# All merge gates of the second block kept in DRAM, their products spread over the three branches' steps

## The chip, the core and the metric

The kernel runs on one core of one Trainium2 chip. The time is device microseconds (us) of one launch: 2844.17 us, the median of 3 runs (2843.86 to 2845.45). The core has a matrix engine (TensorE, PE in the profile; PEld is its weight load), a vector engine (VectorE, DVE), an activation engine (ScalarE, ACT), GpSimd (POOL), and a queue that only issues DMAs (SyncE, SP). Each engine takes its instructions in the order in which they were written into its queue when the program was built, and waits on semaphores for data of the others.

## The reference

A first block (attention, FFN, a linear recurrence, FFN) is followed by a second block of two layers. The change lies in the second block alone. For x of 512 tokens by 1024 channels, each layer computes

```
h = rmsnorm(x, norm_g[l]);  z = h @ w_in[l]
(nsa_q, nsa_kv, nsa_gate, nsa_silu, fox_qkv, fox_f, fox_silu, mem_q, mem_silu, merge_g) = split(z)
o_a = nsa(...) * silu(nsa_silu)        # 8 heads: compressed, selected and window attention
o_b = fox(...) * silu(fox_silu)        # 8 heads: causal attention with a decay
o_m = memory_xattn(...) * silu(mem_silu)   # 4 heads over 256 memory rows
g = sigmoid(merge_g)                   # 3 gates of 512 x 1024
u = g[0] * (o_a @ w_branch_a) + g[1] * (o_b @ w_branch_b) + g[2] * (o_m @ w_branch_m)
x = x + u @ w_out[l]
```

The three gates are one product of h with 3072 columns of w_in; they depend on h alone, not on the branches.

## The kernel before

All products run as three float32r matmuls (`mm3`, L45 to L47): high part by high part, high by low, low by high. A weight tile is loaded from DRAM by SP (`ws`), rounded by ACT (`wh`) and its rest taken by DVE (`wl`), L204 and L212; there are 2 buffers of `ws` and 4 of `wh` and `wl`.

In a layer of the second block three generators run one after the other: `memory`, `nsa` and `fox`. Each yields after a step. `nsa` has 40 steps: 20 blocks of projections, 4 of compressed probabilities, and 16 of heads (one half of the queries of one head each, here called a head step). `fox` has 40 steps too: twice 12 of projections and 8 head steps. In a head step PE computes scores (`sc`, L1160, L1161 in nsa, L1324, L1325 in fox), DVE adds the mask and takes the minimum (L888), ACT the exponential (L889), POOL scales (L891), PE turns the tile (`tr`, L856), ACT and DVE split it (`pt`, L204), and PE multiplies by the values (`pv`, L916). At the end of two heads DVE multiplies by the silu (L940) and the result is split into `o`.

`weave` runs the main generator, and after step n takes as many steps of a filling generator as n stands in the plan (`PLANS`). The filler before is `branch`, one for each branch: a gate's product takes two steps of 12 matmuls (`acc<-hH,wh`, 128x512), then its tanh goes into a tile `mt` in SBUF (L1027; 2 buffers), and one step of 12 matmuls gives one eighth of the branch's output product (`acc<-o,wh`); DVE multiplies it by the gate (L1043, L1046), POOL adds it to `u` (L1047). A branch has 24 filling steps, 72 a layer. A branch's gates and products alternate, so a gate is held in SBUF for a step or two only.

The order written so is not the one in the queues: a scheduler at build time moves an instruction ahead of others whose data are not ready. What stands in the queues is shown below where the change moves it. Products need one of three PSUM banks `acc`; a bank is free when DVE or ACT has read it.

Of the kernel before, what the change touches and what calls it, by code (L numbers as in the profile page):

```python
# [10 lines left out]
F32 = mybir.dt.float32  # L11
# [6 lines left out]
T = 512  # L18
D = 1024
NT = T // 128  # L20
KD = D // 128
# [4 lines left out]
WINDOWS = (128, 512, 2048)  # L26
NB_U = 384
BANKS = {"acc": 3, "sc": 2, "tr": 2, "pv": 1}
SEC_BUFS = {"st": 7, "ws": 2, "w": 4, "o": 6, "P": 5, "pt": 4, "zc": 3, "hst": 4, "fox_t": 4, "of": 2, "rt": 2, "sl": 2, "mt": 2, "cst": 2, "ct": 2}
LRU_BUFS = 24  # L30
NORMALIZE_AFTER, VALUES_AFTER = 5, 6
LRU_STEPS = (0, 1, 2, range(4), "v", 3, range(4, 8), "vvv")
PLANS = ((16,),
         (8, 13, 13, 14, 15, 18, 19, 19, 22, 22, 25, 26, 26, 27, 27, 28, 28, 29, 29, 35, 35, 37, 38, 39),
         (1, 5, 5, 8, 8, 10, 12, 15, 16, 17, 19, 21, 32, 32, 34, 35, 38))
TURN_BANKS = (("acc", "sc"), ("acc", "sc"), ("sc", "tr"), ("tr", "pv"))
TOK_BANKS = (("acc", "acc", "acc", "pv"), ("sc", "sc", "tr", "tr"), ("acc", "acc", "acc", "sc"), ("sc", "tr", "tr", "sc"))

# [4 lines left out]
def mm3(nc, out, lh, ll, rh, rl, start, stop):  # L43

    nc.tensor.matmul(out, lh, rh, start=start, stop=False)  # L45
    nc.tensor.matmul(out, lh, rl, start=False, stop=False)  # L46
    return nc.tensor.matmul(out, ll, rh, start=False, stop=stop)  # L47


@contextmanager  # L50
def behind(tc, *ins):

    with ExitStack() as st:
        for i in ins:
            if i is not None:
                st.enter_context(tc.issue_after(i.ins))
        yield
# [111 lines left out]
class Net:  # L169
# [739 lines left out]
    def pv(self, ps, first, last, v, pts, half):  # L909

        nc = self.nc
        nj = 2 * half + 2
        for j in range(nj):
            lo = 128 if j == nj - 1 else 0
            for u, p in enumerate(pts):
                nc.tensor.matmul(ps[:, lo:256], v(j), p[:, j, lo:], start=first and j == 0 and u == 0, stop=last and j == nj - 1 and u == 1)  # L916

    def merge_halves(self, of, ps, e, half):

# [37 lines left out]
    def second_layer(self, l, z2):  # L957
        nc, i, tc = self.nc, self.i, self.tc
        w_in, h = i["w_in_2"][l], self.h
        with tc.tile_pool(name=f"sec{l}", bufs=1) as self.lp:  # L960
            lp = self.lp
            u, o_m, o_a, o_b = [], [], [], []
            br = [self.branch(l, h, o, i[f"w_branch_{x}_2"][l], b, u) for o, x, b in ((o_m, "m", 2), (o_a, "a", 0), (o_b, "b", 1))]
            self.weave(self.memory(l, h, w_in, z2, o_m), br[0], PLANS[0])
            self.weave(self.nsa(l, h, w_in, o_a), itertools.chain(br[0], br[1]), PLANS[1])
            self.weave(br[0])
            self.weave(self.fox(l, h, w_in, o_b), itertools.chain(br[1], br[2]), PLANS[2])
            self.weave(br[1])
            self.weave(br[2])
            uh = []  # L970
            for k in range(0, KD, 2):
                s = self.state([128, 2, 2, T])
                for q in range(2):
                    self.split(s[:, q, 0], s[:, q, 1], u[k // 4][:, k % 4 + q], scale=0.5)
                uh.append(s)
            lh = lambda k, t: uh[k // 2][:, k % 2, 0, t * 128:(t + 1) * 128]
            ll = lambda k, t: uh[k // 2][:, k % 2, 1, t * 128:(t + 1) * 128]
            last = l == 1
            dst = self.out[0] if last else self.x_new()
            w = i["w_out_2"][l]  # L980
            y0 = list(self.tm(w, 0, 512, lh, ll))
            y1 = self.tm(w, 512, 512, lh, ll, banks=1, tail=4)
            gn = None
            if not last:
                gn = self.lt("o", [128, D])
                nc.sync.dma_start(gn, i["norm_g_2"][l + 1][None, :].to_broadcast([128, D]))

            def new_x(t, *ys):
                xt = self.lt("o", [128, D])
                nc.sync.dma_start(xt, self.x[t * 128:(t + 1) * 128])  # L990
                for c, y in enumerate(ys):
                    cs = slice(c * 512, c * 512 + 512)
                    nc.vector.tensor_tensor(xt[:, cs], xt[:, cs], y, op=OP.add)
# [12 lines left out]
            return gen  # L1006

    def branch(self, l, h, o, w, b, u):

        nc = self.nc  # L1010
        kt = 4
        wv = w.rearrange("(k p) c -> p k c", p=128)
        first = not u
        ts = []

        wg = self.i["w_in_2"][l].rearrange("(k p) c -> p k c", p=128)

        def gate(m):
            c = OFF_MG + b * D + m * 128
            wh, wl = self.wunit(wg[:, :, c:c + 128])  # L1020
            pg = self.bank()
            for k in range(KD):
                mm3(nc, pg, wh[:, k], wl[:, k], h[0][:, k], h[1][:, k], k == 0, k == KD - 1)
                if k == KD // 2 - 1:
                    yield
            t = self.lt("mt", [128, T])
            nc.scalar.activation(t, pg, AF.Tanh, scale=0.5)  # L1027
            ts.append(t)
            yield

        yield from gate(0)
        for m in range(KD):
            if m + 1 < KD:
                yield from gate(m + 1)
            wh, wl = self.wunit(wv[:, :, m * 128:(m + 1) * 128])
            ps = self.bank()
            for k in range(kt):
                mm3(nc, ps, wh[:, k], wl[:, k], o[k][:, 0], o[k][:, 1], k == 0, k == kt - 1)
            t = ts[m]
            if first:  # L1040
                if m % 4 == 0:
                    u.append(self.state([128, 4, T], F32))
                nc.vector.scalar_tensor_tensor(u[m // 4][:, m % 4], t, 1.0, ps, op0=OP.add, op1=OP.mult)  # L1043
            else:
                um = u[m // 4][:, m % 4]
                nc.vector.scalar_tensor_tensor(t, t, 1.0, ps, op0=OP.add, op1=OP.mult)  # L1046
                nc.gpsimd.tensor_tensor(um, um, t, op=OP.add)  # L1047
            yield
# [493 lines left out]
```

## Time and profile before

| what | value |
|---|---|
| median of 3 runs | 2844.17 us |
| the profiled execution | 2847.33 us, of which span 2845.2 us |
| granted TensorE clock, mean | 0.988 |
| PE busy | 2752.4 us (97%) |
| ACT busy | 1285.5 us (45%) |
| DVE busy | 1655.0 us (58%) |
| DMA | 288.52 MB, mean 101 GB/s |

The second block's two layers fill the span from about 1550 us to its end: the first to 2204 us, the second after it. A busy PE is not PE at its full pace: a matmul counts as busy until its last column is out, so short matmuls that wait for each other show little idle time. So the stretches are read by how many matmuls of which size go through in how many us. The column PEclk of the windows is the granted clock: 1.00 is 2.4 GHz, and stretches at half of it run at 1.2 GHz.

### The profile page before, as it was taken

Reading aid. Unit: us, or ns where it says so; the run is one execution under the profiler, and the core shown is the slowest. Engines: PE = TensorE matmul, PEld = TensorE weight load, DVE = VectorE, ACT = ScalarE, POOL = GpSimd, SP = SyncE. Lnnn points to the kernel's source line nnn. Section 1 sums busy time; section 2 is a strip of 40 time slices with the busy share of each in tenths; the row PEclk is TensorE's granted clock in tenths of the full one; section 3 lists DMA queues with packets and bytes.
Section 4 is the critical chain, followed back from the end, with each engine's and each line's share of the span. In section 5 each row is a group of like instructions: output and inputs, shape, how many; then the busy total and the mean of one; then the engine's idle time right before and its main releaser. Section 6 shows DMA issues by size and latency. Waiting matters only on the chain.

```text
span 2845.2 us, 39405 instructions
## 1 busy us (share of the span) xinstructions
PE 2752.4 (97%) x14493; PEld 2338.7 (82%) x14493; DVE 1655.0 (58%) x3306; ACT 1285.5 (45%) x2518; POOL 509.2 (18%) x682
## 2 busy tenths in 40 slices
PE   7999999799999998999998999999999899999999
PEld 6788888688888887888887898789878798788987
DVE  3245555555542678555425687776744677777753
ACT  3234344344432465444323554666533554665542
POOL 0001101111100000111001242333320242333420
PEclk9999999899999999999999999999999999999999
DMA  5553443333332343433323424122234423113233
GB/s 172 171 169 86 104 94 86 118 111 97 97 126 96 112 122 108 126 96 97 126 97 114 125 74 109 38 54 75 71 93 141 137 70 109 34 46 84 71 93 107
DMA packets 386071, 288.52 MB, mean 101 GB/s; under 512 B 33576, under 2 KB 339496, under 8 KB 385880
## 3 DMA queue, kind: packets, MB, share of 16 engines
q1 hardware_dynamic: 376752, 268.94, 32.9%
q10 hardware_dynamic: 9128, 17.07, 1.6%
q8 instruction: 115, 1.88, 0.3%
q14 instruction: 76, 0.62, 0.1%
HBM read 266.86 MB, written 21.20 MB: 101 GB/s over the span
## 4 chain that ended last, share of the span: by engine, by line
PE 82%; DVE 8%; DMA 4%; ACT 3%; issue 2%; POOL 1%; SPq 0%; ACTq 0%; DVEq 0%; POOLq 0%
PE acc L45 20%; PE acc L46 20%; PE acc L47 20%; PE tr L856 2%; PE sc L45 2%; PE sc L46 2%; PE sc L47 2%; DVE wl L204 2%; PE pv L916 2%; PE tr L45 2%; PE tr L47 1%; PE tr L46 1%; PE pv L46 1%; PE pv L47 1%; DMA ws<-in_attn_w_qkv_dram 1%
## 5 line engine op out<-in xcount | busy, mean ns | idle before, releaser
L204 DVE TENSOR_TENSOR wl<-ws,wh 128x1024 fp32r<-128x1024 f32 (+2 forms) x476 | 563.9, 1186 | 686.8 <-ACT wh L204 680.8
L204 ACT CAST wh<-ws 128x1024 fp32r<-128x1024 f32 (+2 forms) x476 | 469.5, 987 | 819.7 <-PE acc L46 303.6
L45 PE MATMUL acc<-hH,wh 128*128 128x512 f32 (+1 forms) x1928 | 742.3, 386 | 12.2 <-ACT gate L769 6.2
L46 PE MATMUL acc<-hL,wh 128*128 128x512 f32 (+1 forms) x1928 | 741.3, 385 | 1.5 <-DVE hL L204 1.2
L47 PE MATMUL acc<-hH,wl 128*128 128x512 f32 (+1 forms) x1928 | 739.5, 384 | 1.0 <-DVE wl L204 1.0
L45 PEld LDWEIGHTS acc<-hH,wh 128*128 128x128 f32 x1928 | 363.3, 189 | 83.6 <-ACT gate L769 6.6
L47 PEld LDWEIGHTS acc<-hH,wl 128*128 128x128 f32 x1928 | 363.9, 189 | 69.2 <-DVE wl L204 1.5
L46 PEld LDWEIGHTS acc<-hL,wh 128*128 128x128 f32 x1928 | 364.1, 189 | 68.4 <-DVE hL L204 2.5
L45 PE MATMUL acc<-wh,hH 128*128 128x256 f32 (+3 forms) x864 | 267.3, 312 | 5.4 <-ACT hH L204 4.1
L46 PE MATMUL acc<-wl,hH 128*128 128x256 f32 (+3 forms) x864 | 266.9, 310 | 2.3 <-DVE wl L204 2.3
L47 PE MATMUL acc<-wh,hL 128*128 128x256 f32 (+3 forms) x864 | 264.9, 309 | 0.1
L45 PEld LDWEIGHTS acc<-wh,hH 128*128 128x128 f32 x864 | 165.6, 192 | 14.5 <-ACT hH L204 4.5
L46 PEld LDWEIGHTS acc<-wl,hH 128*128 128x128 f32 x864 | 165.7, 192 | 11.9 <-DVE wl L204 3.7
L47 PEld LDWEIGHTS acc<-wh,hL 128*128 128x128 f32 x864 | 165.3, 191 | 7.4 <-DVE hL L204 0.4
L645 POOL TENSOR_TENSOR cv<-cv 128x512 f32<-128x512 f32 x48 | 62.0, 1292 | 465.1 <-DVE cv L582 448.4
L582 DVE SCALAR_TENSOR_TENSOR cv<-acc,cw,cv 128x511 f32<-128x511 f32 (+1 forms) x192 | 142.5, 746 | 3.2
L856 PE MATMUL tr<-ident,P 128*128 128x128 f32 x720 | 123.3, 277 | 10.7 <-DVE pt L204 5.2
L817 POOL TENSOR_TENSOR hst<-hst,mhalf 128x4 f32<-128x4 f32 (+2 forms) x90 | 91.0, 1017 | 223.5 <-DVE hst L816 221.7
L889 ACT ACTIVATE P<-P,soft 128x128 f32<-128x128 f32 (+1 forms) x192 | 108.1, 563 | 49.9 <-DVE soft L888 45.7
L888 DVE CUSTOM_DVE_ANT_0 P<-sc,causal 128x128 f32<-128x128 f32 (+1 forms) x192 | 92.9, 486 | 45.8 <-PE tr L856 31.5
L891 POOL TENSOR_SCALAR P<-P,soft,ngate 128x128 f32<-128x128 f32 (+3 forms) x128 | 83.9, 658 | 153.6 <-DVE soft L890 117.5
L204 DVE TENSOR_TENSOR pt<-tr,pt 128x128 fp32r<-128x128 f32 (+2 forms) x224 | 104.1, 474 | 11.8 <-ACT pt L204 10.4
(452 smaller groups left out, 4770.1 us busy)
## 6 DMA issues: line engine op xcount, KB each, us to landing
ws<-in_w_in_dram SPq DMA_DIRECT2D x116, 512.0 KB
ws<-in_ffn_w_up_dram SPq DMA_DIRECT2D x96, 512.0 KB
ws<-in_attn_w_qkv_dram SPq DMA_DIRECT2D x72, 512.0 KB
ws<-in_ffn_w_down_dram SPq DMA_DIRECT2D x48, 512.0 KB
x<-x ACTq DMA_DIRECT2D x16, 512.0 KB
ws<-in_lru_w_in_dram SPq DMA_DIRECT2D x16, 512.0 KB
ws<-in_w_mem_kv_dram SPq DMA_DIRECT2D x16, 512.0 KB
ws<-in_w_out_dram SPq DMA_DIRECT2D x16, 512.0 KB
```

Source lines behind the costliest of these rows:

```text
L45: nc.tensor.matmul(out, lh, rh, start=start, stop=False)
L46: nc.tensor.matmul(out, lh, rl, start=False, stop=False)
L47: return nc.tensor.matmul(out, ll, rh, start=False, stop=stop)
L204: return nc.scalar.copy(hi, src), (eng or nc.vector).tensor_tensor(lo, src, hi.bitcast(F32), op=OP.subtract)
L582: nc.vector.scalar_tensor_tensor(dst[:, s:], ps[:, :T - s], cw(taps - 1 - s), dst[:, s:], op0=OP.mult, op1=OP.add)
L645: nc.gpsimd.tensor_tensor(g, g, v, op=OP.mult)
L817: nc.gpsimd.tensor_tensor(st[:, 1], st[:, 0], self.mhalf[:rows, :nh], op=OP.pow)
L856: self.nc.tensor.transpose(ps[:, a * 128:(a + 1) * 128], s, self.ident)
L888: nc.vector.tensor_tensor_reduce(out=P, in0=S, in1=self.causal[:, 512 - n:512], scale=-1.0, scalar=BIG, op0=OP.add, op1=OP.min, accum_out=m)
L889: nc.scalar.activation(P, P, AF.Exp, bias=m, scale=-1.0, accum_out=s)
L891: nc.gpsimd.tensor_scalar(P, P, r, mult, op0=OP.mult, op1=OP.mult)
L916: nc.tensor.matmul(ps[:, lo:256], v(j), p[:, j, lo:], start=first and j == 0 and u == 0, stop=last and j == nj - 1 and u == 1)
```

## The change

`branch` is cut in two. `gates` computes the 8 pieces of a branch's gate, and after the tanh ACT writes each (256 KB) to a DRAM tensor `gd`. `branch` then reads each back by SP into `mt` (now 3 buffers), one piece ahead, and computes the products. All fillers stand in one chain: gates m, products m, gates a, products a, gates b, products b, and the plans take steps of that chain wherever they stand: 6 during memory, 28 during nsa, 24 during fox. 14 steps are left behind fox (30 before), of which four, two gate pieces, are ordered behind the last value product of fox.

```
-PLANS = ((16,),
+PLANS = ((3, 3, 3, 3, 16, 16),
...
+            self.gd = self.dp.tile([3, KD, 128, T], F32, name=f"gd{l}")
...
+            self.weave(self.memory(l, h, w_in, z2, o_m), fill, PLANS[0])
+            self.weave(self.nsa(l, h, w_in, o_a), fill, PLANS[1])
+            self.weave(self.fox(l, h, w_in, o_b), fill, PLANS[2])
+            with behind(tc, self.last_pv):
+                for n in range(4):
+                    next(fill)
+            self.weave(fill)
...
             nc.scalar.activation(t, pg, AF.Tanh, scale=0.5)
-            ts.append(t)
+            nc.scalar.dma_start(self.gd[b, m], t)
...
+        def load(m):
+            t = self.lt("mt", [128, T])
+            nc.sync.dma_start(t, self.gd[b, m])
+            return t
```

What it does to the queues is shown at three places. PE, last head steps of nsa in the first layer, before (L1160, L1161 scores, L856 turns, L916 and L1171 value products):

```order
L1160 MATMUL sc<-st 128x384
L1161 MATMUL sc<-st 128x384
L916 MATMUL pv<-pt,st 128x256 x6
L916 MATMUL pv<-pt,st 128x128 x2
L856 MATMUL tr<-ident,P 128x128
L1160 MATMUL sc<-st 128x512
L1161 MATMUL sc<-st 128x512
L856 MATMUL tr<-ident,P 128x128 x4
L916 MATMUL pv<-pt,st 128x256 x2
```

The same head steps with the change; the row in L47 is the last of 24 matmuls, and that in L45 the first of 7, of a projection of fox (`acc<-wh,hH`):

```order
L47 MATMUL acc<-wh,hL 128x256
L916 MATMUL pv<-pt,st 128x256
L856 MATMUL tr<-ident,P 128x128 x2
L916 MATMUL pv<-pt,st 128x256
L916 MATMUL pv<-pt,st 128x128 x2
L1181 MATMUL pv<-st,VC 128x256 x2
L856 MATMUL tr<-ident,P 128x128 x3
L45 MATMUL acc<-wh,hH 128x256
```

Products of fox's projection now stand between the turns and the value products, where before only work of the heads stood.

PE, end of the last head of fox in the first layer, before (the rows `acc<-o` are products of a branch):

```order
L916 MATMUL pv<-pt,st 128x256
L916 MATMUL pv<-pt,st 128x128 x2
L856 MATMUL tr<-ident,P 128x128 x4
L45 MATMUL acc<-o,wh 128x512
L46 MATMUL acc<-o,wh 128x512
L47 MATMUL acc<-o,wl 128x512
L916 MATMUL pv<-pt,st 128x256 x6
L916 MATMUL pv<-pt,st 128x128 x2
L45 MATMUL acc<-o,wh 128x512 x2
```

The same place with the change; the last row is the first of 72 gate matmuls (`acc<-hH`), after which all 96 matmuls of the last branch's products follow:

```order
L1334 MATMUL sc<-st 128x512
L1335 MATMUL sc<-st 128x512
L916 MATMUL pv<-pt,st 128x256 x2
L916 MATMUL pv<-pt,st 128x128 x2
L856 MATMUL tr<-ident,P 128x128 x5
L916 MATMUL pv<-pt,st 128x256 x6
L916 MATMUL pv<-pt,st 128x128 x2
L856 MATMUL tr<-ident,P 128x128 x5
L916 MATMUL pv<-pt,st 128x256 x2
L916 MATMUL pv<-pt,st 128x128 x2
L856 MATMUL tr<-ident,P 128x128 x4
L45 MATMUL acc<-hH,wh 128x512
```

Three head steps at the end of fox lost their filling, and gate products took the place behind the last value product.

SP, behind fox in the first layer, with the change (weights of the last branch, and the gates that come back as `mt`):

```order
L994 DMA o<-x_10433 128x1024
L212 DMA ws<-in_w_branch_b_dram 128x4x128 x2
L1038 DMA mt<-gd_11401 128x512 x2
L212 DMA ws<-in_w_branch_b_dram 128x4x128
L1038 DMA mt<-gd_11401 128x512
```

Before, this queue held only loads of weights here; now loads of gates stand between them, in a queue that keeps its order.

## Rows read from the trace of the kernel before

**Rows 1.** The page's span and busy times.
```profile
span 2845.2 us, 39405 instructions
PE 2752.4 (97%) x14493; PEld 2338.7 (82%) x14493; DVE 1655.0 (58%) x3306; ACT 1285.5 (45%) x2518; POOL 509.2 (18%) x682
```

**Rows 2.** Busy times by stretch of the second block, columns in the first row.
```profile
core 0: us, PE busy (x) PEld busy (x) DVE busy (x) ACT busy (x) POOL busy (x), PEclk, DMA share, GB/s
1776.00:1784.00 8.00, 6.51 (x38) 4.83 (x39) 6.85 (x32) 6.80 (x25) 4.46 (x8) 1.00 0.27 66
1784.00:1811.00 27.00, 23.33 (x156) 19.28 (x156) 23.77 (x91) 22.70 (x67) 12.43 (x20) 1.00 0.00 1
1811.00:1880.00 69.00, 68.84 (x449) 62.68 (x449) 43.39 (x129) 39.28 (x102) 18.11 (x26) 1.00 0.21 59
1880.00:1893.00 13.00, 10.42 (x71) 8.39 (x70) 11.08 (x44) 11.26 (x36) 7.33 (x11) 1.00 0.00 0
2086.00:2096.00 10.00, 7.24 (x28) 5.19 (x27) 4.05 (x7) 2.65 (x5) 0.00 (x0) 0.83 0.39 131
2091.00:2095.00 4.00, 4.00 (x10) 2.95 (x11) 0.67 (x1) 0.00 (x0) 0.00 (x0) 0.57 0.17 68
2096.00:2162.00 66.00, 66.00 (x287) 53.73 (x286) 32.34 (x33) 21.64 (x30) 12.18 (x8) 1.00 0.36 105
2430.00:2438.00 8.00, 7.05 (x26) 5.28 (x27) 5.85 (x25) 5.71 (x20) 4.41 (x8) 0.67 0.27 68
2536.00:2550.00 14.00, 11.25 (x71) 8.98 (x70) 11.56 (x44) 11.86 (x38) 7.77 (x12) 0.95 0.01 2
2550.00:2557.00 7.00, 7.00 (x34) 5.85 (x33) 5.27 (x20) 1.92 (x5) 2.35 (x3) 0.85 0.00 0
2742.00:2752.00 10.00, 7.57 (x29) 5.65 (x28) 4.35 (x8) 2.79 (x5) 0.55 (x1) 0.83 0.38 131
```

**Rows 3.** PE's groups by shape, 1880 to 1893 us: count, busy, mean, idle before.
```profile
L856 PE MATMUL tr<-ident,P 128*128 128x128 f32 x25 | 4.5, 277 | 1.9 <-DVE pt L204 1.8
L916 PE MATMUL pv<-pt,st 128*128 128x256 f32 x18 | 4.1, 318 | 0.7 <-ACT pt L204 0.5 <-DVE pt L204 0.2
L916 PE MATMUL pv<-pt,st 128*128 128x128 f32 x10 | 1.7, 251 | 0.0
L1171 PE MATMUL pv<-st,VC 128*128 128x256 f32 x6 | 1.4, 307 | 0.0
L1160 PE MATMUL sc<-st 128*128 128x512 f32 x3 | 1.3, 424 | 0.0
```

**Rows 4.** Timeline around the end of fox, first layer: start, us, instruction, idle before.
```profile
2085.53 0.62 PE L856 MATMUL tr<-ident,P 128*128 128x128 f32 x4
2091.00 0.95 PE L45 MATMUL acc<-o,wh 128*128 128x512 f32 x2 [2.29 <-ACT o L204]
```

**Rows 5.** The page's groups of a head step's chain: busy, mean ns, idle before.
```profile
L889 ACT ACTIVATE P<-P,soft 128x128 f32<-128x128 f32 (+1 forms) x192 | 108.1, 563 | 49.9 <-DVE soft L888 45.7
L888 DVE CUSTOM_DVE_ANT_0 P<-sc,causal 128x128 f32<-128x128 f32 (+1 forms) x192 | 92.9, 486 | 45.8 <-PE tr L856 31.5
L891 POOL TENSOR_SCALAR P<-P,soft,ngate 128x128 f32<-128x128 f32 (+3 forms) x128 | 83.9, 658 | 153.6 <-DVE soft L890 117.5
L204 DVE TENSOR_TENSOR pt<-tr,pt 128x128 fp32r<-128x128 f32 (+2 forms) x224 | 104.1, 474 | 11.8 <-ACT pt L204 10.4
```

**Rows 6.** First attention layer: one ACT copy that waits for an ACT-issued DRAM write.
```profile
66.57 0.59 ACT L442 COPY v<-tr 128x512 f32<-128x512 f32 x1 [2.13 <-DMA vd<-v]
```

**Rows 7.** Instructions by tile: durations min/median/max, first and last start.
```profile
L443 ACTq DMA_DIRECT2D vd<-v x24: 326/326/403, 30.3 to 158.6; - x24
L1046 DVE SCALAR_TENSOR_TENSOR mt<-mt,acc x32: 667/687/690, 1914.5 to 2796.9; 128x512 f32<-128x512 f32 x32
L1047 POOL TENSOR_TENSOR st<-st,mt x32: 1277/1296/2199, 1917.8 to 2797.7; 128x512 f32<-128x512 f32 x32
```

**Rows 8.** The chain of waits: one load of weights, issue to landing.
```profile
1575.22 4.01 DMA ws<-in_w_mem_kv_dram
```

More of the change, by code (lines that the diff above doesn't have):

```diff
@@ L28 @@
 BANKS = {"acc": 3, "sc": 2, "tr": 2, "pv": 1}
-SEC_BUFS = {"st": 7, "ws": 2, "w": 4, "o": 6, "P": 5, "pt": 4, "zc": 3, "hst": 4, "fox_t": 4, "of": 2, "rt": 2, "sl": 2, "mt": 2, "cst": 2, "ct": 2}
+SEC_BUFS = {"st": 7, "ws": 2, "w": 4, "o": 6, "P": 5, "pt": 4, "zc": 3, "hst": 4, "fox_t": 4, "of": 2, "rt": 2, "sl": 2, "mt": 3, "cst": 2, "ct": 2}
 LRU_BUFS = 24
@@ L32 @@
 LRU_STEPS = (0, 1, 2, range(4), "v", 3, range(4, 8), "vvv")
-PLANS = ((16,),
-         (8, 13, 13, 14, 15, 18, 19, 19, 22, 22, 25, 26, 26, 27, 27, 28, 28, 29, 29, 35, 35, 37, 38, 39),
-         (1, 5, 5, 8, 8, 10, 12, 15, 16, 17, 19, 21, 32, 32, 34, 35, 38))
+PLANS = ((3, 3, 3, 3, 16, 16),
+         (8, 8, 12, 13, 14, 16, 18, 19, 20, 21, 22, 23) + tuple(range(24, 40)),
+         (1, 5, 8, 10, 12, 13, 14, 15, 16, 17, 18, 19, 21, 25, 28, 30, 32, 33, 34, 35, 36, 37, 38, 39))
 TURN_BANKS = (("acc", "sc"), ("acc", "sc"), ("sc", "tr"), ("tr", "pv"))
@@ L915, in pv @@
             for u, p in enumerate(pts):
-                nc.tensor.matmul(ps[:, lo:256], v(j), p[:, j, lo:], start=first and j == 0 and u == 0, stop=last and j == nj - 1 and u == 1)
+                self.last_pv = nc.tensor.matmul(ps[:, lo:256], v(j), p[:, j, lo:], start=first and j == 0 and u == 0, stop=last and j == nj - 1 and u == 1)
     def merge_halves(self, of, ps, e, half):
@@ L962, in second_layer @@
             u, o_m, o_a, o_b = [], [], [], []
[L963 to L969, printed above, removed]
+            self.gd = self.dp.tile([3, KD, 128, T], F32, name=f"gd{l}")
+            fill = itertools.chain.from_iterable(
+                (f for b, (o, x) in enumerate(((o_m, "m"), (o_a, "a"), (o_b, "b")))
+                 for f in (self.gates(l, h, (2, 0, 1)[b]), self.branch(o, i[f"w_branch_{x}_2"][l], (2, 0, 1)[b], u))))
+            self.weave(self.memory(l, h, w_in, z2, o_m), fill, PLANS[0])
[5 more added lines that the diff above has]
+            self.weave(fill)
             uh = []
@@ L1006, in second_layer, with gates @@
             return gen
-    def branch(self, l, h, o, w, b, u):
+    def gates(self, l, h, b):
         nc = self.nc
[L1011 to L1014, printed above, removed]
         wg = self.i["w_in_2"][l].rearrange("(k p) c -> p k c", p=128)
-        def gate(m):
+        for m in range(KD):
             c = OFF_MG + b * D + m * 128
@@ L1027, in gate, with branch @@
             nc.scalar.activation(t, pg, AF.Tanh, scale=0.5)
-            ts.append(t)
+            nc.scalar.dma_start(self.gd[b, m], t)
             yield
-        yield from gate(0)
+    def branch(self, o, w, b, u):
+        nc = self.nc
+        kt = 4
+        wv = w.rearrange("(k p) c -> p k c", p=128)
+        first = not u
+        def load(m):
+            t = self.lt("mt", [128, T])
+            nc.sync.dma_start(t, self.gd[b, m])
+            return t
+        ts = [load(0)]
         for m in range(KD):
             if m + 1 < KD:
-                yield from gate(m + 1)
+                ts.append(load(m + 1))
             wh, wl = self.wunit(wv[:, :, m * 128:(m + 1) * 128])
```

## The prediction

> **What bounds the kernel now.** I read the busy times first: PE is busy for 2752.4 of the span's 2845.2 us [rows 1], so time can only be won where PE is short of work, and the change leaves PE's matmuls as they are, moving them. Then the windows, for the pace. Behind fox, where nothing but gates and products runs, 287 matmuls of 512 columns go through in 66 us [rows 2], 0.230 us each, or 0.45 ns a column. In the middle of the heads, 1811 to 1880 us, PE also has work all the time (68.84 of 69 us). In four kinds of place it has not:
>
> - The first heads of nsa, 1776 to 1811 us. DVE is busy for 30.6 of these 35 us and DMA stands nearly still: the heads run alone, at the speed of DVE and ACT.
> - The last heads of nsa, 1880 to 1893 us, the same picture.
> - The end of fox: PE waits 2.29 us for the last head's split [rows 4], and then runs at half clock (0.57 granted from 2091 to 2095 us [rows 2]).
> - The start of memory in each layer. The order of PE, and that of SP for the rows of the memory, is the same there in both kernels, but for two loads of weights. I count nothing.
>
> The shapes tell what is lost in a stretch. 1880 to 1893 us holds 71 matmuls [rows 2]: 25 turns, 18 and 6 value products of 256 columns, 10 of 128, 3 scores of 512, and 9 more, mostly scores [rows 3]. Four turns span 0.62 us with 0.28 for the last alone [rows 3, 4], so one costs 0.11. The sum is 25 x 0.11 + 24 x 0.115 + 10 x 0.057 + 12 x 0.2 = 2.8 + 2.8 + 0.6 + 2.4 = 8.6 us, 0.12 a matmul. So 4.4 of the 13 us are lost.
>
> **The change part by part.**
>
> *Last heads of nsa.* Before, only work of the heads stood there; now 24 and then 7 matmuls of fox's projection stand between turns and value products, about 0.115 us each. Lost before: 4.4 us in the first layer; in the second the same 71 matmuls take 14 us, so 5.4, and 2550 to 2557 us runs at clock 0.85, another 1.0 [rows 2]. What is left where heads are filled I read from 1811 to 1880 us: under 0.2 us idle in 69, so 0.5 a layer with the pipeline's gaps. Gain 4.4 + 5.4 + 1.0 - 1.0 = 9.8 us.
>
> *First heads of nsa.* From 1784 us on nothing changes: five head steps stay bare in the new order too. The second half of `u` needs a buffer that queries of heads 0 to 3 still hold, so finished products keep all three `acc` banks, and no filler can start. Only the entry gets more: products and a silu's matmuls now stand directly ahead of the first head step, and 12 more within it. 1776 to 1784 us holds 38 matmuls, 4.6 us of work at 0.12, so 3.4 are lost; the second layer's 2430 to 2438 us holds 26, 3.1 us, so 4.9 are lost, with clock 0.67 [rows 2]. The 12 inside are 2.8 us, but some of the wait is the chain's own. I take half: 1.7 + 2.4 = 4.1 us. The bounds are 0 and 8.3.
>
> *End of fox.* Here the change takes filling away and adds some. Before, 2086 to 2096 us holds 28 matmuls [rows 2], 8 of them short (0.8 us) and 20 of 0.23: 5.4 us of work, 4.6 lost; the second layer's 29 leave 4.4 lost. The 72 gate matmuls now ordered behind the last value product, 16.6 us, cover the whole path from there over L940 and the split, so all of that goes. In return the last three head steps are bare: 24 value products and 14 turns, 16 x 0.115 + 8 x 0.057 + 14 x 0.11 = 3.8 us of work. At the ratio of the bare stretch of nsa, 13 us for 8.6, this loses 1.9 us; the last value product has only its own split ahead of it, ACT's part and DVE's 0.47 to 0.69, about 1.4 more. So 3.3 a layer. Low bound 1.4, if the chains ran ahead far enough; high bound three whole chains, 0.49 + 0.56 + 0.16 + 0.66 + 0.47 = 2.3 us each [rows 5] (0.16 for the reciprocal is an estimate), 7.0. Net 4.6 + 4.4 - 6.6 = 2.4 us gained; bounds +6.2 and -5.0.
>
> A rule of the Trainium skill speaks against this place: TensorE: Matmul & The Clock Gate, section HAM oscillation, says that a PE which waits between its bursts is throttled again and runs the next burst cold. The trace agrees for the wait of 2.29 us, behind which the clock was 0.57 [rows 2, 4]; it does not for the 27 bare us from 1784, whose waits are shorter and whose clock stayed 1.00. By the rule each bare end would cost some 1.7 us more (half of the 3.4 us that the 0.57 over 4 us makes at half clock), and the sum would be 3.4 us smaller.
>
> *The way through DRAM.* It adds 24 writes on ACT and 24 reads on SP a layer. ACT's issue of such a write takes 0.33 us [rows 7]: 48 x 0.33 = 15.8 us of ACT, which is 45% busy; a gate's tanh stands where PE has filler, and none is issued in the bare first heads. So nothing of it is on the path. A tanh must also wait until the write three gates back has landed. The nearest row is the first layer's values, where one copy of 24 waited 2.13 us on such a write [rows 6]; two of 48 would be 4.3 us. On the other side, a read that comes late stops DVE at the gate's multiplication and everything behind it, the splits of weights and of heads. A product's round is: DVE 0.69, POOL 1.30 [rows 7], which frees the buffer, then SP's issue and 4.0 us to land, taking a load of twice the bytes [rows 8]: 6.0 us, and three buffers allow three products, 3 x 2.76 = 8.3 us. So it is hidden with 2.3 us to spare. DMA was 36% busy behind fox at 105 GB/s [rows 2]; 512 KB in 2.76 us are 190 GB/s, some 65%. From below: moving gates out of branches can't shorten the products, so 0. I take 3.5 us for all of it, nearest to the row that waits, with 0 and 30 (below) as ends.
>
> *The tail.* 30 steps before, 14 now; the 16 others, 16 x 12 x 0.23 = 44 us of PE work, now stand in the heads and projections. That alone is worth nothing: PE was dense in the tail, and the time comes back only where it was short of work, the places above. Eight products in a row need 0.69 us of DVE for the gate and up to 1.3 of weights and `u` each, in 2.76.
>
> Sum: 9.8 + 4.1 + 2.4 - 3.5 = 12.8 us gained. The profiled execution took 2847.3 us, 2.1 more than its span and 3.2 more than the median; none of the terms lies outside the span, so 2834.5 by it and 2831.4 against the median. I predict 2831 us.
>
> **The rivals.**
>
> *The gain is given back at new bare places* (time within 0.2%). For it: filling inside the heads is no greater than before, only elsewhere; what fills the last heads of nsa is taken from fox's projections, whose turns wait for POOL. Against it: those projections have gate products beside them. With 3 us more lost there a layer, the high bound at the end of fox (7.4 more) and the entry at 0 (4.1 less), the 12.8 become -4.7: 2849 at worst; more likely half of these, 2840.
>
> *Reads of gates hold up the weights* (slower). In SP's queue a read that waits for POOL's addition of three products back stands ahead of weights. In fox's heads POOL also scales the heads, so an addition comes late, the weights behind the read land late, and PE stands. Five reads of each of the last two branches wait so, 20 in all. It decides from 0.64 us of delay each (12.8 / 20); at 1.5 us each it costs 30, and the time is 2844 + 30 - 12.8 = 2861. Against it: weights are loaded two to three units ahead, 5.5 to 8 us, and POOL was busy for 17.5 of 36 us even in bare heads [rows 2], less elsewhere. The Trainium skill, DMA: Bandwidth & Descriptors, section Issuing engines are not separate DMA queues, has writes issued on ACT interleave with SP's loads on the same DMA engines; no row here shows what that costs a load.
>
> *More is recovered.* Both half-clock stretches of the second layer go, the entry is wholly covered, and the ends lose only 1.4: 9.8 + 8.3 + 6.2 = 24 us, 2820.
>
> **How the numbers follow.** A change under 0.2%, 5.7 us, is what a measurement can't tell from none: 2838.5 to 2849.9. The forecast, a gain of 6 to 20 us, gets 0.60; more recovered 0.07; given back 0.19; weights held up 0.14. So faster 0.67, same 0.19, slower 0.14. The forecast's own range is 2824 to 2838. The range for 8 in 10 starts at 2820 and reaches over most of the given-back case, to 2848; most of the slower case is left out.
>
> **What would show it.** Right: in the last heads of nsa 71 matmuls of heads stand in a stretch that PE fills; the wait for the split of `o` is gone from the end of fox, and the three bare steps take about 7 us; five bare head steps remain near the first heads, with the same 27 us. Wrong: DVE's multiplication by the gate idle before it on a DMA of `mt`; SP waiting for POOL with weights behind; a clock below 1 behind the end of fox; or bare turns in fox's projections.

## The result, and the profile after

The changed kernel takes 2863.48 us (median of 4 runs, 2861.38 to 2865.98) where the kernel before, beside it, took 2844.02: the ratio is 1.0068, with a 95% interval of 1.0051 to 1.0086. It is 19 us slower, not 13 us faster. Its profiled execution took 2864.05 us, 16.7 more than that of before. The page's first rows answer to [rows 1]; the same 14493 matmuls keep PE busy for 10.8 us longer:

```profile
span 2862.2 us, 39548 instructions
PE 2763.2 (97%) x14493; PEld 2348.0 (82%) x14493; DVE 1648.6 (58%) x3306; ACT 1290.1 (45%) x2518; POOL 519.8 (18%) x682
```

To see where the time goes I took, in each trace, the start of every matmul to the start of the next, less the pace of a dense stretch (0.443 ns a column, 0.109 us a turn; both kernels run at it behind fox). What is left is PE's loss, waits and half clock together. Summed over stretches of the second block, both layers, in us (worked out from the traces, no row of a view):

```
                     ahead of   compressed  nsa heads  nsa heads  nsa heads  fox up to    fox's   rest   all
                     the probs  probs       0, 1       2, 3       4 to 7     its end      end
before                  7.8        5.6        13.2       13.7       19.0       16.9       12.2    32.7  121.2
the change             16.7       14.2        19.2       13.3        9.0       16.3       21.6    27.9  138.2
e1_swap                18.7        5.4         2.2        3.2       29.2       31.2       19.0    29.0  137.8
e2_nobehind            16.8       14.5        19.0       13.3        9.0       16.3        6.6    28.0  123.7
e3_dram                 8.9        5.7        10.1       14.6       23.9       14.2        2.8    32.2  112.4
t2_swap_hold           33.8       19.9         9.1        8.5       16.9       35.9        5.8    26.9  156.9
d1_mt3                  8.3        5.6         9.6       14.9       23.9       18.0       12.6    33.0  125.9
d2_w2s                  9.3       14.5        19.4       13.3        9.0       16.3       19.6    27.1  128.6
w1_spread               8.3        5.5         2.4        6.6       23.9       14.6       20.2    28.4  110.0
u1_two_undone           9.5       14.5        20.0       13.7        9.0       16.3        6.6    27.5  117.2
w4_lag3                12.9       10.3        12.8        5.8       12.8       44.5       11.0    27.1  137.4
x1_gates_at_probs       8.3        5.4         6.7       16.5       22.2       14.5        6.6    27.9  108.2
f2_hold_last_piece     17.0       14.2        19.0       13.3        9.0       16.4        8.0    27.8  124.6
```

"Ahead of the probs" are the 70 us before the first score of the compressed probabilities (`sc<-KC,st`), "nsa heads 4 to 7" end with the last product of the compressed values, fox's end is the 330 matmuls from its last score on (some 270 in w1_spread, which leaves fewer steps behind fox), "rest" is what remains of the block. About 5.3 us in the column of the probs are the method's own in every row: a score there has 64 columns, 0.028 us by the pace, but in dense stretches too they start 0.11 us apart. The change loses 17.0 us more than before, which is the difference of the two spans. It lost less at the last heads of nsa (10.0) and in the rest (4.8, most of it in memory, which now has six filling steps), and more at three places: 8.9 ahead of the probs, 14.6 at the probs and the first two heads, 9.4 at the end of fox.

The windows of the changed kernel, first layer, in the columns of [rows 2]:

```profile
1721.00:1731.00 10.00, 9.55 (x62) 8.95 (x62) 6.47 (x11) 4.67 (x10) 0.00 (x0) 0.83 0.53 153
1762.80:1773.40 10.60, 7.09 (x49) 6.23 (x47) 9.67 (x29) 4.29 (x9) 0.62 (x1) 1.00 0.31 86
1776.00:1784.00 8.00, 7.61 (x28) 5.96 (x27) 7.09 (x25) 3.08 (x9) 2.93 (x6) 0.73 0.39 113
1806.00:1833.00 27.00, 24.06 (x159) 19.89 (x158) 23.95 (x88) 21.93 (x66) 12.71 (x20) 1.00 0.02 2
1906.00:1919.00 13.00, 13.00 (x104) 12.65 (x103) 10.47 (x31) 9.67 (x23) 3.32 (x5) 1.00 0.31 84
2099.00:2112.00 13.00, 9.77 (x45) 7.70 (x45) 7.96 (x19) 6.53 (x17) 1.28 (x2) 0.71 0.36 123
2112.00:2120.00 8.00, 8.00 (x31) 6.45 (x30) 1.65 (x3) 1.74 (x3) 0.00 (x0) 0.83 0.01 2
2120.00:2186.00 66.00, 66.00 (x286) 53.43 (x285) 31.65 (x37) 19.21 (x27) 13.94 (x9) 1.00 0.51 159
```

A stretch of nsa's last heads (1906) is now full: 104 matmuls in 13 us, where 71 stood before. The five bare head steps (1806) are as they were, 159 matmuls in 27 us. The tail (2120) has the old pace. The new losses are the other windows.

**At the compressed probabilities** PE is busy for 7.09 of 10.6 us. The same stretch of the kernel before was full:

```profile
1752.60:1765.90 13.30, 13.30 (x78) 11.53 (x77) 11.49 (x36) 6.89 (x12) 2.74 (x4) 1.00 0.31 82
```

There, mostly gate matmuls stood between the groups of eight scores. Now the products of branch m do, and PE's timeline of the changed kernel ends them early (start, us, instruction, idle before):

```profile
1767.38 0.40 PE L47 MATMUL acc<-o,wl 128*128 128x512 f32 x1
1767.62 1.97 PE L1258 MATMUL sc<-KC,st 128*128 128x64 f32 x16
1772.06 1.05 PE L1258 MATMUL sc<-KC,st 128*128 128x64 f32 x8 [2.48 <-DVE P L1261]
```

DVE's timeline shows why no further product follows the one that ended at 1767.8:

```profile
1776.31 0.29 DVE L888 CUSTOM_DVE_ANT_0 P<-sc,causal 128x128 f32<-128x128 f32 x1 [0.20 <-PE tr L856]
1776.52 0.08 DVE L888 DVE_READ_ACCUMULATOR2_ANT soft<- 128x1 f32 x1
1776.52 1.88 DVE L1053 SCALAR_TENSOR_TENSOR st<-mt,acc 128x512 f32<-128x512 f32 x3
```

Three products are read in one go at 1776.5, behind the first head's minimum: until then they held all three `acc` banks, while DVE was busy for 9.67 of 10.6 us with the probabilities. A gate leaves its bank by ACT's tanh, and ACT was 4.29 of 10.6 us busy. Part of the loss is the clock: behind the wait it is 0.73 from 1776 to 1784 us. In both layers' probs and first two heads 17.1 us run at half clock, where before 6.8 did, all in the second layer; the matmuls started in them are worth 6.0 and 3.0 us at full pace. So some 3 of the 14.6 us are the clock's, an estimate from the starts and the clock records of the two traces.

**Ahead of the probabilities** one late weight is the cause. In the kernel before, the same small weight was issued and cast within 1.7 us (SP, then ACT):

```profile
1695.64 0.35 SPq L212 DMA_DIRECT2D ws<-in_cmp_w_k_dram  x1
1697.31 0.25 ACT L204 CAST wh<-ws 128x64 fp32r<-128x64 f32 x1 [0.49 <-DMA ws<-in_cmp_w_k_dram]
```

Timelines of SP, ACT and PE of the changed kernel:

```profile
1706.62 0.35 SPq L212 DMA_DIRECT2D ws<-in_cmp_w_k_dram  x1
1715.85 6.61 SPq L212 DMA_DIRECT2D ws<-in_w_in_dram  x3
```

```profile
1713.69 0.76 ACT L847 CAST st<-tr 64x256 fp32r<-64x256 f32 x2 [1.87 <-DVE st L850]
1714.62 0.25 ACT L204 CAST wh<-ws 128x64 fp32r<-128x64 f32 x1
1719.69 1.04 ACT L204 CAST wh<-ws 128x1024 fp32r<-128x1024 f32 x1 [2.10 <-DMA ws<-in_w_in_dram]
```

```profile
1720.79 1.01 PE L45 MATMUL acc<-wh,hH 128*128 128x256 f32 x3 [2.48 <-ACT wh L204]
```

The small weight of the compression (128x64) is issued at 1706.62 and holds one of the two `ws` buffers until its cast at 1714.62, which stands in ACT's queue behind a cast of a query (L847) that waited for DVE. The next weight is issued 9.2 us after it, and PE waits 2.48 us and then runs at clock 0.83 over 10 us.

**At the end of fox** PE's timeline shows the three bare head steps:

```profile
2101.73 0.30 PE L856 MATMUL tr<-ident,P 128*128 128x128 f32 x1 [1.29 <-DVE pt L204]
2102.89 1.53 PE L916 MATMUL pv<-pt,st 128*128 128x256 f32 x8 [0.87 <-ACT P L889]
2108.19 2.48 PE L916 MATMUL pv<-pt,st 128*128 128x256 f32 x8 [0.68 <-ACT pt L204]
2110.47 0.73 PE L45 MATMUL acc<-hH,wh 128*128 128x512 f32 x1
```

Eight value products take 1.53 us, then 2.48: the clock has fallen, to 0.71 over 2099 to 2112 us. It is still 0.83 in the 8 us after, when gates keep PE busy all the time. The stretch at half clock by itself:

```profile
2104.50:2114.80 10.30, 9.37 (x31) 7.34 (x30) 4.31 (x8) 3.11 (x7) 0.00 (x0) 0.50 0.15 54
```

The eight value products at 2108.19 stand between the last four turns and the first gate; the printed order of the changed kernel leaves them out.

**The way through DRAM** holds up no engine. Rows by tile of the changed kernel: duration of the issue (min/median/max), and issue to landing:

```profile
L1026 ACTq DMA_DIRECT2D gd<-mt x48: 326/326/357, 1578.0 to 2792.1; - x48
DMA to landing us min/median/max: 2.0/2.2/4.3
```

```profile
L1038 SPq DMA_DIRECT2D mt<-gd x48: 319/339/1001, 1751.0 to 2807.9; - x48
DMA to landing us min/median/max: 2.6/3.2/4.3
```

DVE's multiplication by the gate waits for PE's product, not for `mt` (8.4 us idle before its 32 instances, 7.6 of it ended by PE):

```profile
L1056 DVE SCALAR_TENSOR_TENSOR mt<-mt,acc 128x512 f32<-128x512 f32 x32 | 21.8, 683 | 8.4 <-PE acc L47 7.6
```

The other 16, of branch m (L1053), waited 2.0 us, for PE alone, and no tanh waited for a write. The reads did wait in SP's queue for a buffer of `mt` (us in total, times, longest):

```profile
SPq L1038 <- DVE st L1053: 68.9, 6, 28.5
```

The two longest (28.5 and 28.4 us) lie in the bare heads, one a layer; the first ended at 1831.69, and the next weight went out at 1836.93. PE waited for no weight there.

### The profile page after: what moved, and what is told of

Same layout as the page of the kernel before. It is cut to its first block, busy times and chain, and to the rows that moved or that the text cites. A ratio compares the mean times of both kernels' runs of the same rounds, so it can differ in the third digit from the quotient of the medians.

```text
span 2862.2 us, 39548 instructions
## 1 busy us (share of the span) xinstructions
PE 2763.2 (97%) x14493; PEld 2348.0 (82%) x14493; DVE 1648.6 (58%) x3306; ACT 1290.1 (45%) x2518; POOL 519.8 (18%) x682
## 4 chain that ended last, share of the span: by engine, by line
PE 85%; DVE 7%; DMA 4%; ACT 2%; issue 2%; POOL 1%; SPq 0%; ACTq 0%; DVEq 0%; POOLq 0%
PE acc L45 21%; PE acc L46 21%; PE acc L47 21%; PE tr L856 3%; PE pv L916 2%; PE sc L45 2%; PE sc L46 2%; PE sc L47 2%; DVE wl L204 2%; PE tr L45 1%; PE tr L47 1%; PE tr L46 1%; PE pv L46 1%; PE pv L47 1%; PE pv L45 1%
## 5 line engine op out<-in xcount | busy, mean ns | idle before, releaser
L204 DVE TENSOR_TENSOR wl<-ws,wh 128x1024 fp32r<-128x1024 f32 (+3 forms) x476 | 564.8, 1188 | 715.5 <-ACT wh L204 710.0
L204 ACT CAST wh<-ws 128x1024 fp32r<-128x1024 f32 (+3 forms) x476 | 469.8, 987 | 805.0 <-PE acc L46 299.1
L45 PE MATMUL acc<-hH,wh 128*128 128x512 f32 (+1 forms) x1928 | 743.0, 386 | 10.2 <-ACT gate L769 6.2
L47 PE MATMUL acc<-hH,wl 128*128 128x512 f32 (+1 forms) x1928 | 741.1, 385 | 1.0 <-DVE wl L204 1.0
L45 PEld LDWEIGHTS acc<-hH,wh 128*128 128x128 f32 x1928 | 363.9, 189 | 79.9 <-ACT gate L769 6.6
L47 PEld LDWEIGHTS acc<-hH,wl 128*128 128x128 f32 x1928 | 364.5, 189 | 69.7 <-DVE wl L204 1.8
L45 PE MATMUL acc<-wh,hH 128*128 128x256 f32 (+3 forms) x864 | 269.2, 313 | 11.6 <-ACT wh L204 4.5
L47 PE MATMUL acc<-wh,hL 128*128 128x256 f32 (+3 forms) x864 | 265.4, 309 | 0.0
L45 PEld LDWEIGHTS acc<-wh,hH 128*128 128x128 f32 x864 | 166.8, 193 | 22.1 <-ACT wh L204 5.2
L47 PEld LDWEIGHTS acc<-wh,hL 128*128 128x128 f32 x864 | 166.4, 193 | 7.0
L856 PE MATMUL tr<-ident,P 128*128 128x128 f32 x720 | 124.8, 278 | 4.2 <-DVE pt L204 3.8
```

The source lines that it names most:

```text
L204: return nc.scalar.copy(hi, src), (eng or nc.vector).tensor_tensor(lo, src, hi.bitcast(F32), op=OP.subtract)
L856: self.nc.tensor.transpose(ps[:, a * 128:(a + 1) * 128], s, self.ident)
```

## The experiments

Each ratio is against the kernel before, measured beside it on the same chip (its median was 2840.3 to 2846.1 us from chip to chip). Differences in us are differences of ratios times 2844.

| run | ratio, 95% interval | against | us |
|---|---|---|---|
| the change | 1.0068, 1.0051 to 1.0086 | before | +19.3 |
| e1_swap | 1.0071, 1.0057 to 1.0085 | the change | +0.9 |
| e2_nobehind | 1.0018, 1.0008 to 1.0027 | the change | -14.2 |
| e3_dram | 0.9974, 0.9965 to 0.9984 | before | -7.4 |
| t2_swap_hold | 1.0132, 1.0118 to 1.0146 | before | +37.5 |
| d1_mt3 | 1.0033, 1.0021 to 1.0046 | before | +9.4 |
| d2_w2s | 1.0029, 1.0018 to 1.0040 | the change | -11.1 |
| w1_spread | 0.9968, 0.9955 to 0.9980 | before | -9.1 |
| u1_two_undone | 0.9995, 0.9987 to 1.0004 | the change | -20.8 |
| w4_lag3 | 1.0083, 1.0068 to 1.0098 | before | +23.6 |
| x1_gates_at_probs | 0.9966, 0.9953 to 0.9978 | u1_two_undone | -8.2 |
| f2_hold_last_piece | 1.0019, 1.0010 to 1.0029 | the change | -13.9 |

**e1_swap: gates of a ahead of the products of m** (the chain in words).

```
-  gates m, products m, gates a, products a, gates b, products b
+  gates m, gates a, products m, products a, gates b, products b
```

> One edit to the changed kernel: in the chain of fillers the gates of branch a come before the products of branch m (gates m, gates a, products m, products a, gates b, products b). Plans, DRAM way and the four steps behind fox's last value product stay. Theory A (what stands beside the compressed probabilities and the first heads of nsa decides: products need the buffer of u and DVE, which reads them out behind the work of the heads, while gates need only h and leave their bank by ACT): gate matmuls now fill that place, so most of the roughly 23 us that PE loses there in each layer between the first compressed score and the fifth head goes, but the same filling is then missing at the last heads of nsa, where about four head steps become bare and lose 7 to 9 us. Net 10 to 13 us a layer: about 2840 us (2832 to 2846). Theory B (the way through DRAM holds up weights and tanh): nothing of that is changed, so the time stays within 3 us of the changed kernel, 2860 to 2866.

Theory A was right on the place and wrong on the sum: the time can't be told from that of the change. The first four heads and the probs lost 10.8 us instead of 46.7, and the last four heads 29.2 instead of 9.0, fox, mainly its first projection, 14.9 more. The stretch in which the last heads end and the next, at fox's first turns (columns as before):

```profile
1919.00:1929.50 10.50, 7.44 (x50) 6.22 (x49) 9.18 (x30) 6.31 (x17) 6.54 (x8) 0.95 0.00 1
1929.50:1940.00 10.50, 3.46 (x19) 2.96 (x18) 7.29 (x23) 3.64 (x8) 5.38 (x5) 0.66 0.04 6
```

The number of filling steps did not change; used at the first heads, they are gone at the last, which stand bare.

**e2_nobehind: nothing ordered behind fox's last value product.**

```
-            with behind(tc, self.last_pv):
-                for n in range(4):
-                    next(fill)
```

> One edit to the changed kernel: the four filling steps behind fox's last value product are no longer ordered behind it; they are left to the scheduler, which puts 5 gate pieces' matmuls between the turns and value products of the last three head steps. Theory A (the bare heads at the end of fox lose what the trace shows there, 9 to 11 us, of which the wait for the split of o is no part any more): the heads are filled again, the wait for the split of o comes back with its stretch at half clock, and the end of fox loses 5 to 6 us a layer as in the kernel before; 8 to 10 us faster than the changed kernel, about 2854 us. Rival (the end of fox was bound by the chain of the heads in any case, and filling only lengthens it): no gain, 2860 to 2868.

14.2 us, more than expected: fox's end loses 3.3 us a layer, not 5 to 6. It stays at full clock:

```profile
2107.00:2120.00 13.00, 12.88 (x71) 10.72 (x69) 4.31 (x8) 4.77 (x10) 0.00 (x0) 1.00 0.37 110
```

**e3_dram: the kernel before, with the way through DRAM and its three buffers of `mt`** (cut; `load` is that of the change).

```
-... "mt": 2, ...
+... "mt": 3, ...
...
             nc.scalar.activation(t, pg, AF.Tanh, scale=0.5)
-            ts.append(t)
+            nc.scalar.dma_start(self.gd[b, m], t)
...
+                ts.append(load(m + 1))
```

> The kernel before with the way through DRAM alone: each gate's tanh goes to DRAM by ACT and comes back by SP one piece ahead of its product, with three buffers of mt; fillers and plans are in the order of the kernel before. Theory A (the order costs the time, not DRAM): within 4 us of the kernel before, 2842 to 2848. Theory B (DRAM way costs it): 10 to 20 us slower, 2854 to 2864.

Neither: it is 7.4 us faster than before. Theory B falls, and with it, for this order of the fillers, the rival that reads hold up the weights; DVE waited for a gate's read twice, 2.8 us together. The gain is at fox's end (12.2 to 2.8): in PE's queue 24 gate matmuls now stand right behind the last value product, where in the kernel before the product that waits for the split of `o` stood. The first of them:

```profile
2080.54 1.45 PE L916 MATMUL pv<-pt,st 128*128 128x256 f32 x8
2081.83 0.45 PE L45 MATMUL acc<-hH,wh 128*128 128x512 f32 x1
```

In the 10 us from its last eight value products on, 47 matmuls go through at full clock, where [rows 2] had 28 in 2086 to 2096 us:

```profile
2080.50:2090.50 10.00, 9.86 (x47) 7.98 (x46) 4.61 (x7) 3.35 (x6) 0.00 (x0) 1.00 0.55 184
```

**t2_swap_hold: e1_swap, with each filling step ordered behind the value product one head step back.**

```
+            held = [pvs[-2]] if len(pvs) > 1 else []
+            for _ in range(sum(p == n for p in plan)):
+                with behind(self.tc, *held):
+                    next(fill, None)
```

> The chain of e1_swap, and in nsa and fox each filling step's matmuls are ordered on TensorE behind the last value product of the head step before (for the compressed probabilities: behind the last score matmul of the step before), so that filling can't run ahead of the heads and be missing later. Order on TensorE alone; loads, casts and splits are free to run ahead. Theory A (time is lost only where heads stand bare, and there is filling enough for each head step to have 12 matmuls, 2.7 us, against the 1.9 us that a bare head step loses): nearly all of the loss of the first heads of nsa (16 to 23 us a layer) and of its last heads (1 to 5) goes and half of that at the end of fox: 25 to 45 us faster than the changed kernel, 2820 to 2838 us. Rival C (clumps of 12 matmuls behind each head step delay the turns and scores queued behind them, and with them DVE and ACT, so the heads' chain only gets longer): 2845 to 2865.

Slower than all: rival C is nearer in time, and its range too low. Its mechanism is not what the table shows: the heads of nsa lost less than before (34.5 against 45.9), and the loss is elsewhere, 33.8 ahead of the probs and 35.9 in fox, where I take it that the held filling was missing. At the probs the clock fell as well:

```profile
1750.60:1775.20 24.60, 23.12 (x100) 19.03 (x99) 15.42 (x51) 7.43 (x15) 3.69 (x6) 0.78 0.22 65
```

**d1_mt3: the kernel before with `"mt": 3`.**

> The kernel before with one number changed: three buffers of mt instead of two, no DRAM. It separates the two parts of e3_dram, which was 8 us faster than the kernel before, 9 to 10 of it at the end of fox. Theory A (the third buffer lets the gate after next be multiplied while two others wait for their products, so gate matmuls stand between the last value product of fox and the product that waits for the split of o): the same gain, 2832 to 2837 us, and the end of fox loses under 2 us. Theory B (the gate's way out of SBUF gives it): no change, 2840 to 2844, and the end of fox loses 5 to 6.5 us.

The end of fox loses 12.6 as before, so Theory B holds there: not the third buffer but the way through DRAM changed the order. The buffer alone makes the kernel 9.4 us slower, so the way through DRAM is worth more than e3_dram's 7.4. In the table it costs 4.7, at the last heads of nsa (19.0 to 23.9, as in e3_dram). More can't be asked of these two traces: the profiled execution of d1_mt3 was 2.7 us below its median, that of the kernel before 3.2 above its own. Why the buffer changes the last heads is open.

**d2_w2s: a buffer of its own for the small weights.**

```
-        ws = self.wp.tile(shape, F32, tag="ws", bufs=SEC_BUFS["ws"], name="ws")
+        small = shape[0] == 128 and shape[1:] == [64]
+        ws = self.wp.tile(shape, F32, tag="w2s" if small else "ws", bufs=1 if small else SEC_BUFS["ws"], name="ws")
```

> The changed kernel with a buffer of its own for the two small weights (128x64) of the compression's second product, which before took one of the two ws buffers. In the changed kernel that small load stands in a ws buffer for 8 us (issued at 1706.6, its cast at 1714.6 behind head work in ACT's queue), the next weights are issued at 1715.9 and PE waits 2.5 us for their cast and then runs at half clock. Theory A (that is what the 4 to 5 us more before the first compressed score in each layer are): 6 to 10 us faster than the changed kernel, 2852 to 2856 us, and that stretch loses 4 to 5 us as in the kernel before. Rival (PE is short of filling there, and the weights are late only because nothing else is): no gain, 2859 to 2864.

Theory A: 16.7 falls to 9.3, the time by 11.1 (9.6 in the table). The stretch at full clock:

```profile
1712.00:1732.00 20.00, 19.31 (x148) 17.51 (x147) 13.04 (x27) 10.02 (x24) 4.22 (x7) 1.00 0.45 123
```

2.0 us of the 9.6 came at the end of fox, which the edit leaves alone. There the first layer shows the same three bare steps at full clock nearly to their end; it fell for 3.4 us only, while PE was busy all the time:

```profile
2093.80:2106.80 13.00, 9.24 (x48) 7.25 (x47) 8.29 (x20) 6.98 (x18) 1.28 (x2) 0.87 0.39 123
2103.30:2106.70 3.40, 3.40 (x12) 2.92 (x12) 1.20 (x3) 0.98 (x2) 0.00 (x0) 0.50 0.02 5
```

This end loses 8.9 us, the second layer's, with 10.24 us at half clock, 10.8 as in the change. The 3.4 us cost 1.7, so 7.2 us of the loss are waits and would be there without any half clock. Why the clock came back sooner here is open.

**w1_spread: a first version meant to beat both** (chain gates m, gates a, products m, gates b, products a, products b; nothing held; own small buffer):

```
-         ... + tuple(range(24, 40)),
-         (1, 5, 8, 10, 12, 13, 14, 15, 16, 17, 18, 19, 21, 25, 28, 30, 32, 33, 34, 35, 36, 37, 38, 39))
+         ... + tuple(range(24, 40)) + tuple(range(32, 40)),
+         (1, 5, 8, 10, 12, 13, 14, 15, 16, 17, 19, 21, 32, 33, 34, 35, 36, 37, 39))
```

> A version meant to beat both: chain gates m, gates a, products m, gates b, products a, products b; nothing ordered behind fox's last value product; own buffer for the small weights; 8 more filling steps in the last eight head steps of nsa and 5 fewer in fox, so that 11 are left behind fox. Theory A (bare heads move to wherever filling is short; with enough of it in nsa the 20 us a layer that the changed kernel loses between the first compressed score and the end of nsa fall to 8 to 10, its end of fox from 10.8 to 5 to 7, the stretch before the compressed probabilities by 4): 18 to 20 us a layer faster than the changed kernel, about 2824 us (2815 to 2836). Rival (what is filled in nsa is bare in fox, as e1_swap moved it from the first heads to the last): 2840 to 2860.

It beats both, inside Theory A's range. But fox's end still loses 20.2: its last head steps are bare, and as all gates are used up by then, the product behind the last value product waits for the split of `o` as in the kernel before:

```profile
2111.70 0.79 PE L45 MATMUL acc<-o,wh 128*128 128x512 f32 x1 [2.29 <-ACT o L204]
```

**u1_two_undone: e2_nobehind and d2_w2s together.**

> The changed kernel with the two single edits together that each made it faster: nothing ordered behind fox's last value product (e2_nobehind, 15 us), and a buffer of its own for the compression's small weights (d2_w2s, 11 us). Theory A (two separate losses, in different stretches): they add, 2834 to 2838 us, and what is left above the kernel's other stretches is the loss at the compressed probabilities and the first heads. Rival (the stretches share the same scarce filling, so what one gains the other loses, as between the first and last heads in e1_swap): 2842 to 2848.

At their own places the two add (16.7 to 9.5 and 21.6 to 6.6). In time they give 20.8 of 25.3 us: 2842.6 us at 2844 for the kernel before, in the rival's range by its number. The table names part of what is short: the 2.0 us that d2_w2s won at the end of fox are won by e2_nobehind already.

**w4_lag3: filling held three head steps back.**

```
+            held = [pvs[-4]] if len(pvs) > 3 else []
```

> A version meant to beat both: chain gates m, gates a, products m, products a, gates b, products b; own buffer for the small weights; 6 more filling steps in the heads of nsa and 6 fewer in fox; in the heads a filling step's matmuls are ordered on TensorE behind the last value product three head steps back (t2_swap_hold: one back, in clumps of 12); behind fox only the last gate piece (two steps) is ordered behind the last value product. Theory A (filling enough for every head step, free to go into the gaps of three head steps, but not further): nsa from the first compressed score to its end loses 10 us a layer (w1_spread: 18 to 19), the end of fox 3 to 5 (10), the stretch before the probabilities 5: 2805 to 2820 us. Rival C (holding filling back costs as in t2_swap_hold, where the stretch up to the first head lost 26 us): 2835 to 2860.

Rival C again, and beyond its range. Nsa's probs and heads fell to 41.7 us (before: 51.5), but fox lost 44.5, some 21 of it with its first set of heads and 15 with the second, which starts at 2065.5 us:

```profile
2065.00:2080.00 15.00, 11.79 (x54) 9.49 (x53) 11.41 (x36) 11.04 (x30) 3.97 (x7) 0.89 0.44 119
```

So my theory that filling held back and spread evenly is best is not borne out: neither version that holds it back gains. That the holding is the cause is not shown for w4_lag3, which also moved six filling steps from fox to nsa.

**x1_gates_at_probs: u1_two_undone, with three gate pieces of a ahead of the products of m** (the chain in words).

```
-  gates m, products m, gates a, ...
+  gates m, gates a 0 to 2, products m, gates a 3 to 7, ...
```

> u1_two_undone with one more edit: three gate pieces of branch a (6 filling steps) stand in the chain ahead of the products of branch m, the other five behind them. Plans and number of filling steps stay. So gate matmuls stand beside the compressed probabilities, and the products of branch m come 6 steps later. Theory A (products there wait for DVE, which reads them out of the three PSUM banks behind the heads' work, while gates leave by ACT): from the first compressed score to the third head PE loses 6 to 9 us a layer instead of 16.9, the rest of nsa the same 11 or up to 4 more (bare steps at its end), so 8 to 16 us faster than u1_two_undone, about 2833 us against a kernel before of 2844. Rival (filling is what is scarce, not the kind of it: e1_swap lost at the end what it won at the start): within 4 us of u1_two_undone.

At the probs and the first two heads 12.1 us are lost instead of 34.5, 6 a layer as Theory A said; the rest of nsa gives back 16 of these 22 (expected up to 8). The probabilities run full:

```profile
1760.10:1773.20 13.10, 13.10 (x79) 11.45 (x77) 10.48 (x41) 4.19 (x11) 2.47 (x4) 1.00 0.61 182
```

With 0.9966 this is the fastest version measured, 9.7 us ahead of the kernel before; w1_spread can't be told from it.

**f2_hold_last_piece: only the last gate piece held behind the last value product.**

```
+            for n in range(4):
+                next(fill)
             with behind(tc, self.last_pv):
-                for n in range(4):
+                for n in range(2):
                     next(fill)
```

> One edit to the changed kernel: of the 14 filling steps behind fox the first four are left free and the two after them (the last gate piece, 24 matmuls instead of 72) are ordered behind the last value product. Theory A (each bare head step at the end of fox costs 2 to 3 us, and with three of them PE also falls to half clock; one piece is enough to cover the split of o): one bare step instead of three, no half clock, the end of fox loses 2 to 4 us a layer instead of 10.8, so 13 to 17 us faster than the changed kernel, at or a little below e2_nobehind (3.3 us lost there). Rival (the cost of the end is the order behind the last value product itself, which delays whatever follows): half of that, 6 to 9 us.

Theory A: 4.0 us lost a layer, one bare step, and the clock stays up:

```profile
2107.00:2120.00 13.00, 11.56 (x65) 9.68 (x64) 5.01 (x9) 4.28 (x9) 0.00 (x0) 1.00 0.59 188
```

## Why the prediction was wrong

- **Last heads of nsa**, predicted +9.8: the difference is right, 10.0. The last four heads lost 19.0 and now 9.0, both over a longer stretch than the one I priced.
- **First heads of nsa**, predicted +4.1 with bounds of 0 and 8.3: this step failed, by 18.7 us. I read the entry from 1776 us on, saw more matmuls ahead of it and took them for a gain. The stretch just before, the compressed probabilities, was dense (78 matmuls in 13.3 us) and had no term; the change took its gates away and put products there. Which filling stands somewhere decides what it needs: the prediction itself knew that finished products keep the `acc` banks, and used it only for the heads after. x1_gates_at_probs shows it: 22.4 us back at this place with gates in front, of which later heads took 16.
- **End of fox**, predicted +2.4, from 6.6 lost in six bare steps: measured -9.4. What I counted as gone did go (gates follow at once, at 2110.47), the bare steps are mis-sized: I put the loss at 3.3 us a layer, and it was 10.8, the three steps 11 us instead of 7. Most of the miss is waits: 7.2 us without the clock, by the first layer of d2_w2s, about my high bound of three whole chains, 7.0. The ratio of nsa's bare heads was no measure: there PE's longest wait was 0.7 us, here 1.29 and 0.87. The rest, 3.6, is the clock, which was left out of the sum: 10.24 us a layer at half clock. The prediction had set the rule of the Trainium skill (TensorE: Matmul & The Clock Gate, section HAM oscillation) against the 27 bare us whose clock stayed 1.00, and kept the row. At this place the trace agrees with the rule, with about twice the 1.7 us that I gave it. The bare heads of nsa still run 159 matmuls in 27 us at 1.00, the end of fox 45 in 13 us at 0.71. "A clock below 1 behind the end of fox" was among my signs of being wrong. Why the waits are longer there is open.
- **No term at all** for the stretch ahead of the probabilities, 8.9 us. "In four kinds of place it has not" counted where PE was short before; the change made a fifth, by moving where the small weight's cast stands in ACT's queue. d2_w2s shows the cause.
- **The way through DRAM**, predicted -3.5: no cost found in the changed kernel, and on the kernel before it is a gain of 7.4 us with its third buffer (e3_dram), through the order at fox's end, which the prediction had not looked for in the tail.
- **Memory and the rest**, no term: 4.8 us were gained there, a miss in my favour.
- **The rivals.** The measured time is near that of "reads hold up the weights" (2861), by chance and not by its mechanism: no read of a gate held up DVE, and the one late weight waited for a `ws` buffer. "Given back at new bare places" names the kind; its price, 17.5 us at worst (12.8 gained to 4.7 lost), was too small for a swing of 32. The three losses together are 32.9 us, less 14.8 gained at the last heads and in memory.

With the two losses undone and gates in front of the probabilities, 0.9966 is a gain of 9.7 us. That it is near the 12.8 of the sum doesn't bear the sum out: its terms differ.

## What to carry to other kernels

When filling is moved, cost the places it leaves and the places between, not only the bare ones it goes to: a stretch that is dense before may be dense because of what stands there. Ask of each filler which engine frees its PSUM bank, and whether that engine is the one that the work beside it needs. A buffer that small and large loads share holds the large ones up for as long as the small one's consumer is late (8.0 us here).

## What the runs showed of the hardware

Bare heads need not cost the same: 27 us with 159 matmuls kept clock 1.00, 13 us with 45 fell to 0.71, and the 8 us of unbroken matmuls after were at 0.83. Nor does one place: the same end of fox had 3.4 us at half clock in one layer of d2_w2s and 10.24 in the other. 48 writes and 48 reads of 256 KB through DRAM landed in 2.2 and 3.2 us (medians), and no engine of the changed kernel waited for one, though reads waited up to 28.5 us in SP's queue for their buffer. Open: why a third buffer of `mt` alone costs 9.4 us, and why the scheduler puts a gate behind fox's last value product once gates come back from DRAM.
